# Both feed-forward openings and the second tail put under the list schedule of a decoder layer on one core

## The chip, the cores and the metric

The kernel runs on one core of one Trainium2 chip. The metric is the device time of one execution in microseconds (us). Engines are called TensorE (PE, with its weight loads PEld), VectorE (DVE), ScalarE (ACT), GpSimd (POOL) and SyncE (SP, which issues the DMAs).

## What is computed

One layer on 16 meta tokens and 1024 tokens of width 1024: a half-step SwiGLU feed-forward, a mixing stage, a second half-step feed-forward and a last norm. The core of the reference:

```python
h = h + 0.5 * swiglu(rmsnorm(h, norm_ffn1[l]), w_ffn1_gate[l], w_ffn1_up[l], w_ffn1_down[l])
u = rmsnorm(h, norm_mix[l])
qa, ka, va, qi, ki, wi, qs, ksw, vsw, ga, gb = jnp.split(u @ w_in[l], IN_SPLITS, axis=-1)
...
o_sparse = sparse_branch(qa, ka, va, qi, ki, wi, pos, kvalid, topk)
o_swa = swa_branch(qs, ksw, vsw, sinks[l], pos, kvalid)
merged = (jax.nn.sigmoid(ga) * (o_sparse @ w_branch_sparse[l])
          + jax.nn.sigmoid(gb) * (o_swa @ w_branch_swa[l]))
h = h + merged @ w_out[l]
h = h + 0.5 * swiglu(rmsnorm(h, norm_ffn2[l]), w_ffn2_gate[l], w_ffn2_up[l], w_ffn2_down[l])
return rmsnorm(h[:, BLOCK:], norm_final)

def swiglu(x, w_gate, w_up, w_down):
    return (jax.nn.silu(x @ w_gate) * (x @ w_up)) @ w_down
```

The feed-forward width is 2816, in 22 chunks of 128.

## The kernel before, in words

Activations lie transposed: eight tiles of 128 channels, the tokens in two halves x = 0 (528 columns, the 16 meta tokens among them; in the second feed-forward 512) and x = 1 (512 columns). Every float32 operand of a matmul is split into a high and a low half-precision part (`split_w` for weights, `norm_u` for the normalised rows u): ScalarE makes the high part, VectorE subtracts for the low part, and `mm3` sums three products of parts.

The function `ffn` makes one feed-forward stage. Its first pair of chunks is projected directly by `plain_pair(0)`: four weights (two gates, two ups), each by eight u tiles, for x = 0 and then x = 1; between the first halves it calls `other_half`, the norm of x = 1. From then on pairs of chunks are done with a Strassen-Winograd scheme: seven block products of half the depth (`fast`) instead of eight. Weights are combined by `wide_weights` or, for later jobs, step by step by `prepare`; the t blocks (`make_t`, `combine`) are four combinations of the normalised rows and their splits, made from rows that are computed again (`gained`) or kept (`saved`); the sixteen differences are on GpSimd. The product list `UP` is p1, p6, p7, p5, c11, p74, p53: p1 and c11 and p53 use blocks of u, the others t blocks t1 to t4. `gate_part` evicts a gate's seven products (`half_products`), `up_part` those of the up weights; `combine` on GpSimd and `split_later` make the hidden blocks for the down products. `passes` are the last projections of a stage, each followed by squares, norm and (in the second stage) the output.

In the first stage the whole of x = 0 is loaded, squared (ScalarE, added by VectorE), normalised and split; x = 1 is squared on GpSimd.

Order: the class `Plan` (a list schedule) records the operations between `start` and `run`, books each with a cost (`cost`), and issues them in planned order on the four compute engines; where it is off, operations are issued as the program says, inside a `manual_schedule` block in that order. An item's priority is its place in the program plus `shift`. Before the change only the mixing stage is planned, from `to_mix` (the last projections of the first stage included) to line 1430. `add` marks an operation as `shared` if it has two float32 inputs in SBUF; while GpSimd works such an item on VectorE is booked 0.4 us longer. Tiles in PSUM (`whole`) count as one piece for dependencies. A buffer of a ring comes free in the plan with the last use in program order.

## Time and profile before

| | us |
|---|---|
| median of 3 runs | 2007.55 (2007.2 to 2009.01) |
| the profiled execution | 2009.06 |
| its span, first to last instruction | 2007.3 |
| TensorE busy | 1922.9 (96%) |
| VectorE busy | 1630.3 (81%) |
| ScalarE busy | 898.2 (45%) |
| GpSimd busy | 385.1 (19%) |
| mean granted TensorE clock | 0.988 |

The table of stretches gives the busy time of each engine between two moments; a stretch's length minus TensorE's busy time is the time in which TensorE stood still. Groups of instructions give busy time, the mean of one and the idle time before them with what ended it. In the timeline a row is one run of like instructions: start, duration of the run, count. A duration of several matmuls holds the pipelined end of the last one, so the distance of two starts is the better price.

### The profile page before, as it was taken

The page shows a single profiled execution, that of the slowest core. Times are in us where ns is not written, and L with a number is a line of the kernel's source. Part 1 is how long each engine was busy: PE and PEld are TensorE (multiplying, and loading weights), DVE is VectorE, ACT ScalarE, POOL GpSimd, SP SyncE. Part 2 cuts the span into 40 slices and gives each one's busy share as a digit, 9 for nine tenths or more (in the row PEclk, how much of TensorE's full clock was granted, in tenths as well). Part 3 has the DMA queues.
Part 4 walks back from the last instruction along what each step waited for, and adds up shares of the span by engine and source line. Part 5 has one row for each costly group of instructions (what it writes and reads, how often), then busy time and mean ns, then how long its engine had stood idle before and what let it go on. Part 6 is the DMA issues. An engine that isn't in the chain of part 4 may idle for free.

```text
span 2007.3 us, 32840 instructions
## 1 busy us (share of the span) xinstructions
PE 1922.9 (96%) x13080; PEld 1201.4 (60%) x13080; DVE 1630.3 (81%) x2787; ACT 898.2 (45%) x1602; POOL 385.1 (19%) x313
## 2 busy tenths in 40 slices
PE   5899999999998999999999999998899999999997
PEld 4588888888887655655555656444344444444443
DVE  7988778788774899999998977566987888788767
ACT  4434233333322455669887555434333333243232
POOL 4511312221220033131000000002322213312200
PEclk9899999999999999999999999999999999999998
DMA  4011111211121554221111231341112111211213
GB/s 160 11 54 58 59 64 38 69 64 59 48 85 38 190 160 149 69 91 64 32 48 43 85 102 52 105 147 42 43 38 68 63 58 48 64 63 48 79 37 131
DMA packets 58873, 146.95 MB, mean 73 GB/s; under 512 B 7264, under 2 KB 13408, under 8 KB 58720
## 3 DMA queue, kind: packets, MB, share of 16 engines
q1 hardware_dynamic: 58720, 144.86, 22.6%
q8 instruction: 102, 1.67, 0.3%
q14 instruction: 51, 0.42, 0.1%
HBM read 130.01 MB, written 14.76 MB: 72 GB/s over the span
## 4 chain that ended last, share of the span: by engine, by line
PE 79%; DVE 12%; ACT 5%; issue 2%; DMA 1%; POOL 1%; SPq 0%; DVEq 0%; ACTq 0%; POOLq 0%
PE pc L188 15%; PE pd L188 15%; PE pa L188 15%; PE pb L188 7%; PE p_gate L326 7%; PE p_out L326 4%; PE p_br L326 3%; PE pdn L188 2%; PE ptr L326 2%; PE rp L326 2%; ACT jk L326 1%; PE pdn L326 1%; PE pv_b L326 1%; DVE wsp L326 1%; DVE sc L326 1%
## 5 line engine op out<-in xcount | busy, mean ns | idle before, releaser
L188 PEld LDWEIGHTS <-wsp 128*128 128x128 f16 x4848 | 478.0, 99 | 293.2 <-issue 30.9
L188 PEld LDWEIGHTS <-x 128*128 128x128 f16 x3132 | 307.2, 98 | 156.5 <-issue 7.0
L326 PEld LDWEIGHTS <-wsp 128*128 128x128 f16 x2448 | 235.8, 99 | 223.0 <-issue 6.9
L188 PE MATMUL pa<-u,wsp 128*128 128x264 f16 (+1 forms) x1440 | 224.7, 310 | 0.0
L326 PE MATMUL p_gate<-u,wsp 128*128 128x512 f16 x768 | 188.4, 379 | 0.0
L188 POOL TENSOR_TENSOR h<-h,base 128x512 f32<-128x512 f32 (+1 forms) x72 | 116.3, 1615 | 291.1 <-DVE base L188 229.7
L326 PE MATMUL rp<-u,wsp 128*128 128x512 f16 (+2 forms) x624 | 140.2, 366 | 4.0 <-DVE rt L326 3.7
L188 ACT ACTIVATE wsp<-wst 128x1024 f16<-128x1024 f32 (+2 forms) x88 | 80.4, 915 | 142.3 <-DMA wst<-in_wd_dram 50.4
L326 DVE SCALAR_TENSOR_TENSOR wsp<-wst,wsp 128x1024 f16<-128x1024 f32 (+2 forms) x104 | 107.5, 1036 | 27.3 <-ACT wsp L326 27.0
L188 PE MATMUL pb<-tb,wsp 128*128 128x264 f16 (+1 forms) x720 | 114.0, 312 | 8.7 <-ACT tb L188 5.9
L188 PE MATMUL pc<-tb,x 128*128 128x264 f16 (+1 forms) x720 | 114.0, 313 | 5.1 <-DVE c L188 5.0
L326 ACT ACTIVATE wsp<-wst 128x1024 f16<-128x1024 f32 (+2 forms) x104 | 91.1, 880 | 58.4 <-PE p_out L326 16.4
L188 PE MATMUL pc<-tb,wsp 128*128 128x256 f16 (+1 forms) x720 | 113.6, 313 | 0.0
L188 PE MATMUL pd<-u,x 128*128 128x256 f16 (+1 forms) x720 | 110.7, 308 | 0.0
L188 PE MATMUL pd<-tb,x 128*128 128x256 f16 (+1 forms) x720 | 110.7, 308 | 0.0
L188 POOL TENSOR_TENSOR t<-g,g 128x512 f32<-128x512 f32 x16 | 25.5, 1592 | 434.4 <-DVE g L188 434.4
L188 ACT ACTIVATE wsp<-sa 128x1024 f16<-128x1024 f32 (+1 forms) x64 | 62.3, 973 | 101.4 <-DVE sa L188 101.2
L326 ACT ACTIVATE jk<-sc,s5nb 128x784 f16<-128x784 f32 (+2 forms) x93 | 98.1, 1055 | 15.9 <-DVE s5nb L326 13.1
L188 PE MATMUL pa<-hid,wsp 128*128 128x264 f16 (+1 forms) x648 | 103.1, 310 | 0.0
L188 PE MATMUL pd<-hid,x 128*128 128x256 f16 (+1 forms) x648 | 101.6, 308 | 0.0
L188 DVE TENSOR_TENSOR c<-pc,base 128x512 f32<-128x512 f32 x80 | 55.4, 692 | 55.1 <-PE pc L188 54.8
L188 ACT ACTIVATE base<-pa 128x528 f32<-128x528 f32 (+1 forms) x64 | 38.2, 598 | 133.6 <-PE pa L188 133.6
(218 smaller groups left out, 3494.7 us busy)
## 6 DMA issues: line engine op xcount, KB each, us to landing
wst<-in_wgu_dram SPq DMA_DIRECT2D x88, 512.0 KB, 3.8
wst<-in_win_dram SPq DMA_DIRECT2D x44, 512.0 KB, 3.5
wst<-in_wd_dram SPq DMA_DIRECT2D x48, 384.0 KB, 3.5
wst<-in_wd_dram SPq DMA_DIRECT2D x32, 256.0 KB, 2.8
wst<-in_wout_dram SPq DMA_DIRECT2D x16, 512.0 KB, 3.7
qscr<-ry SPq DMA_DIRECT2D x20, 256.0 KB, 2.1
q<-qscr SPq DMA_DIRECT2D x20, 256.0 KB, 3.1
wst<-in_wbs_dram SPq DMA_DIRECT2D x16, 256.0 KB, 3.2
```

The source lines that it names most:

```text
L188: return getattr(engine.real, op)(*[give(a) for a in args], **{k: give(v) for k, v in kw.items()})
L326: getattr(engine.real, op)(*[give(a) for a in args], **{k: give(v) for k, v in kw.items()})
```

## The change

- The first stage gets a new opening, `first_pair`: three slices of tokens (272 and 256 columns of x = 0, then x = 1), each with its own squares (all on ScalarE, added on VectorE), norm and u; the four weights of the first pair take turns at every u tile; the normalised rows stay in their tiles and become the t blocks by differences on VectorE. The first slice of every h tile is loaded first, then the first weight, the second slices, the other weights (two of them into tiles of the weight sums), then x = 1.
- The first gate part of both stages is `first_gate` with the list `FIRST`: p1, p3, c11, p7, p5, p6, p74, where p3 (the product that was p53) has a bank of its own. Its evictions run with a shift of -200.
- The first stage is planned from its start to the end of that gate part; the second stage is planned from its start to the end of its first gate part, and again from its last projections to the end.
- The first two weights of the second stage are loaded and split at the end of the mixing plan (`pre`).
- The planner: `shared` counts every input that isn't a column, the surcharge is 0.5 us; matmuls into disjoint parts of one PSUM tile don't depend on each other; a buffer comes free when all its uses are done.
- A norm's Newton step is three operations instead of four.

The diff, cut:

```diff
@@ class Plan, add
-        shared = sum(v.dt == F32 and not v.base.whole for v in ins) > 1 and not any(v.base.whole for v in ins)
+        shared = sum(v.shape[1:] != (1,) for v in ins) > 1 and not any(v.base.whole for v in ins)
@@ class Plan, run
             if e == "DVE" and shared and pool_till > t:
-                busy, done = busy + 0.4, done + 0.4
+                busy, done = busy + 0.5, done + 0.5
@@ layer_kernel
     open_phase("ffn1")
     ph["S"] = 2
+    nc.start()
...
-    load_h(0)
+    CUT = 272
+    for k in range(KD):
+        nc.sync.dma_start(h[0][k][:, :CUT], xT[k][:, :CUT])
...
+    def newton(r, e, a):
+        nc.vector.scalar_tensor_tensor(e, r, -0.5, r, op0=ALU.mult, op1=ALU.mult)
+        nc.vector.tensor_mul(e, e, a)
+        nc.vector.scalar_tensor_tensor(r, e, 1.5, r, op0=ALU.add, op1=ALU.mult)
...
+        def first_products(m, blocks, first, done):
+            for what, ps in urgent(joint(blocks, FIRST)):
...
+                elif what == "p3":
+                    c12 = ftmp("c12")
+                    nc.scalar.activation(vb(c12), ps, AF.Copy)
...
+                elif what == "p5":
+                    nc.vector.tensor_add(vb(c22), ps, vb(c22))
+                    nc.vector.tensor_add(vb(c12), ps, vb(c12))
+                elif what == "p6":
+                    nc.vector.tensor_add(vb(c22), ps[:, :, :wb], vb(c22))
+                    done(3, c22, vb(c22))
+                    nc.vector.tensor_add(va(base), ps, va(base))
+                    nc.vector.tensor_add(vb(c12), va(base)[:, :, :wb], vb(c12))
...
+        def first_pair():
+            sl = ((0, 0, 272), (0, 272, 528), (1, 0, 512))
...
+            def norm_part(s, k):
...
+                nc.vector.scalar_tensor_tensor(t, hs[x][k][:, c0:c1], g_all[:, gi, k:k + 1], rb[s],
+                                               op0=ALU.mult, op1=ALU.mult)
+                nc.scalar.activation(u[x][k][:, 0, c0:c1], t, AF.Copy)
+                nc.vector.tensor_sub(u[x][k][:, 1, c0:c1], t, u[x][k][:, 0, c0:c1])
...
+            def matmuls(s, order):
...
+                for k in order:
+                    for i in range(4):
+                        mm3(ps[i // 2][:, i % 2, :width[s]], sp[i], slice(k * P, (k + 1) * P), u[x][k],
+                            slice(c0, c1), k == order[0], k == order[-1])
...
+            for i in range(4):
+                t1 = ftmp("t1")
+                a1, b1, a2, b2 = un[0][i], un[1][i], un[0][i + 4], un[1][i + 4]
+                nc.vector.tensor_sub(vb(t1), vb(b1), va(a1)[:, :, :wb])
+                nc.vector.tensor_sub(vb(b1), vb(b2), vb(b1))
+                nc.vector.tensor_sub(va(a1)[:, :, :wb], vb(b2), vb(t1))
+                nc.vector.tensor_sub(va(a2), va(a2), va(a1))
...
+        FIRST = ("p1", "p3", "c11", "p7", "p5", "p6", "p74")
+        if u is None:
+            vals, u, t_blocks = first_pair()
+            parts = [first_gate]
+        else:
+            vals = plain_pair(0)
+            parts = [first_gate]
...
-                        gates = gate_part(blocks)
+                        gates = (parts.pop() if parts else gate_part)(blocks)
+                        if nc.on:
+                            nc.run(keep=...)
...
+    raws = [load_raw(wgu1[0], 1024)]
     for k in range(KD):
+        nc.sync.dma_start(h[0][k][:, CUT:], xT[k][:, CUT:HS0[1]])
+    raws.append(load_raw(wgu1[1], 1024))
+    for i in (2, 3):
+        raws.append(new(ph["sb"], [P, 1024], F32, tag="wS", name="wst", bufs=2))
+        nc.sync.dma_start(raws[i], wgu1[i])
+    for k in range(KD):
+        nc.sync.dma_start(h[1][k], xT[k][:, HS0[1]:])
...
-    nc.run(early=6.0, keep=h2[0] + h2[1] + u3[0] + rb3 + [acc])
+    pre += [load_w(wgu2[i], 1024) for i in range(2)]
+    nc.run(early=6.0, keep=pre + h2[0] + h2[1] + u3[0] + rb3 + [acc])
     close_phase()
     open_phase("ffn2")
     ph["S"] = 1
+    nc.start()
...
-    acc = ffn(u3, rb3, h2, 2, wgu2, wd2, lambda: ffn2_norm(1, acc), passes, saved2, lambda: None)
+    acc = ffn(u3, rb3, h2, 2, wgu2, wd2, lambda: ffn2_norm(1, acc), passes, saved2, nc.start)
     x, subs, done = passes[-1]
     done(norm_stats(acc, subs))
+    nc.run(early=6.0)
```

## Rows read from the trace of the kernel before

**Rows 1.** Stretches: start:end, length, busy PE, PEld, DVE, ACT, POOL (count), clock, DMA, GB/s

```profile
0.00:114.65 114.65, 78.69 (x493) 54.98 (x494) 97.34 (x130) 52.27 (x84) 51.84 (x39) 0.94 0.24 84
...
628.00:674.00 46.00, 40.19 (x310) 30.96 (x308) 26.37 (x54) 15.20 (x27) 0.95 (x1) 0.93 0.37 117
674.00:1000.00 326.00, 309.46 (x2277) 182.35 (x2276) 315.17 (x807) 219.47 (x524) 71.64 (x77) 0.99 0.32 104
...
1359.30:1439.10 79.80, 67.77 (x292) 30.78 (x292) 65.34 (x78) 34.94 (x53) 31.62 (x20) 0.91 0.10 33
...
sum 2007.30, PE 1922.93 PEld 1201.45 DVE 1630.27 ACT 898.20 POOL 385.12; mean PE 240.37 PEld 150.18 DVE 203.78 ACT 112.28 POOL 48.14
```

**Rows 2.** Waits of PE to 115 us: in total, times, longest

```profile
PE nsum L188 <- DVE acc L188: 11.4, 1, 11.4
PE nbc L188 <- DVE n_r L188: 8.0, 2, 4.2
PE pg L188 <- DVE u L188: 6.5, 7, 2.3
```

**Rows 3.** VectorE groups by shape, to 115 us: busy us, mean ns

```profile
L188 DVE TENSOR_TENSOR u<-un,u 128x512 f16<-128x512 f32 x8 | 9.7, 1265 | 0.0
L188 DVE SCALAR_TENSOR_TENSOR wsp<-wst,wsp 128x1024 f16<-128x1024 f32 x6 | 8.9, 1484 | 0.0
L188 DVE TENSOR_TENSOR u<-un,u 128x272 f16<-128x272 f32 x8 | 8.1, 1021 | 0.1
L188 DVE TENSOR_TENSOR tb<-tu,tb 128x528 f16<-128x528 f32 x8 | 7.3, 913 | 0.5 <-ACT tb L188 0.3
L188 DVE SCALAR_TENSOR_TENSOR tu<-h,g_all,rb 128x528 f32<-128x528 f32 x8 | 5.8, 758 | 0.0
...
L188 DVE TENSOR_TENSOR acc<-acc,sq 128x528 f32<-128x528 f32 x7 | 5.0, 708 | 5.5 <-ACT sq L188 5.1
L188 DVE SCALAR_TENSOR_TENSOR tu<-h,g_all,rb 128x512 f32<-128x512 f32 x4 | 4.9, 1250 | 0.0
L188 DVE TENSOR_TENSOR tb<-t,tb 128x512 f16<-128x512 f32 x4 | 4.1, 1019 | 1.4 <-ACT tb L188 1.2
...
L188 DVE TENSOR_TENSOR u<-un,u 128x256 f16<-128x256 f32 x8 | 3.3, 419 | 0.1
...
L188 DVE SCALAR_TENSOR_TENSOR wsp<-sa,wsp 128x1024 f16<-128x1024 f32 x2 | 2.4, 1215 | 0.0
```

**Rows 4.** Timeline of VectorE: start us, us, instruction, count

```profile
72.91 0.68 DVE L188 TENSOR_TENSOR tb<-un,tb 128x512 f16<-128x512 f32 x1
```

**Rows 5.** Timeline of all engines, head of the first opening

```profile
0.74 3.93 SPq L188 DMA_DIRECT2D h<-in_xT_dram  x8
...
20.17 0.38 PE L188 MATMUL pg<-u,wsp 128*128 128x264 f16 x1 [0.20 <-ACT u L188]
```

**Rows 6.** Waits of PE in the second opening, 1359 to 1440 us

```profile
PE pb L188 <- ACT tb L188: 2.6, 1, 2.6
PE nbc L188 <- DVE n_r L188: 2.4, 1, 2.4
PE pc L188 <- DVE c L188: 2.3, 1, 2.3
```

**Rows 7.** Timeline of PE, second opening: like matmuls at two clocks

```profile
1365.24 5.34 PE L188 MATMUL pu<-u,wsp 128*128 128x512 f16 x24
...
1380.85 7.25 PE L188 MATMUL pu<-u,wsp 128*128 128x512 f16 x24
```

**Rows 8.** Table of stretches within the second opening

```profile
1359.30:1381.00 21.70, 18.51 (x89) 9.96 (x89) 9.23 (x17) 7.86 (x10) 0.00 (x0) 0.93 0.15 51
...
1400.00:1421.85 21.85, 17.70 (x79) 7.67 (x78) 21.70 (x21) 8.60 (x13) 12.98 (x8) 0.93 0.08 25
```

**Rows 9.** Timeline of PE, first opening: like matmuls at two clocks

```profile
28.11 0.86 PE L188 MATMUL pg<-u,wsp 128*128 128x264 f16 x3
...
35.71 1.96 PE L188 MATMUL pg<-u,wsp 128*128 128x264 f16 x16
```

More of the change, by code (lines that the diff above doesn't have):

```diff
@@ L112, in __init__ @@
         self.seen = []
-        self.last = self.first = None
+        self.first = None
+        self.uses, self.till = [], 0.0
     def real(self):
@@ L201, in add @@
                 for j, other, wrote in b.seen:
-                    if (write or wrote) and j != i and overlap(box, other):
+                    if (write or wrote) and j != i and (overlap(box, other) or b.whole and not (
+                            engine.name == "PE" == self.items[j][0].name)):
                         deps.add(j)
-                if write and box is None:
+                if write and (box is None or b.whole and engine.name != "PE"):
                     b.seen = []
@@ L242, in run @@
         for b in tiles.values():
-            if id(b) not in kept and b.last is not None:
-                dies[b.last].append(b)
+            if id(b) not in kept:
+                b.left = len(b.uses)
+                for i in b.uses:
+                    dies[i].append(b)
         for q in queues.values():
@@ L316, in run @@
             for b in dies[i]:
-                if b.key in free:
-                    free[b.key].append(end + 0.1)
+                b.left, b.till = b.left - 1, max(b.till, end + 0.1)
+                if b.key in free and not b.left:
+                    free[b.key].append(b.till)
                     grant(b.key)
@@ L864, in ffn @@
                     if f < NF - 2:
-                        gates = gate_part(blocks)
+                        gates = (parts.pop() if parts else gate_part)(blocks)
+                        if nc.on:
+                            nc.run(keep=hs[0] + hs[1] + u[0] + u[1][4:] + sum(t_blocks, []) + [ident, ones, g_all]
+                                   + [t for t, _ in gates] + [t for t, _ in weights[1]] + fetched[2]
+                                   + sum(down, []))
                 if not last:
```

168 lines of the change are left out of this document (133 added, 35 removed).

## The prediction

> **What bounds the kernel now.** I read the table of stretches first. TensorE works 1922.9 of the 2007.3 us (its last row), so a change of order can give back at most the 84 us in which it stands still, and the table says where these are [rows 1]: 114.65 - 78.69 = 36.0 us in the opening of the first feed-forward stage (from the start to the first product of the up part), 46.00 - 40.19 = 5.8 us where that stage passes into mixing, 326.00 - 309.46 = 16.5 us in the first half of mixing, 79.80 - 67.77 = 12.0 us in the opening of the second feed-forward stage. That is 70.3, all but some 14 us, which lie almost wholly behind the last projection. The reader is to see in the same rows that VectorE is busy 97.34 of 114.65 us in the first opening and 315.17 of 326 us in the first half of mixing: there TensorE waits because VectorE is full.
>
> Next, what TensorE waits for in the first opening [rows 2]: 11.4 us for the summed squares, 8.0 us in two waits for the inverse norm, 6.5 us for the low halves of u; all are VectorE's results. Then VectorE's work by shape [rows 3]. The point there is that one operation has two prices: the subtraction that makes the low half of u takes 419 ns at 256 columns and 1021 ns at 272, 1265 ns at 512 columns, while a subtraction of the same size elsewhere took 0.68 us [rows 4]. The dear ones lie where GpSimd works too (51.84 us in this stretch, [rows 1]): it makes the squares of the second half of the tokens and the sixteen differences for the t blocks.
>
> **First opening.** VectorE is its clock, so I keep a ledger of VectorE.
>
> Taken away. The normalised rows stay in their tiles and the t blocks are made from them, so the twelve operations that compute them again go: 5.8 + 4.9 = 10.7 us [rows 3]. GpSimd leaves this stretch but for four differences of the first hidden pair, so the surcharge goes: 8 x (1.265 - 0.68) = 4.7, 8 x (1.021 - 0.42) = 4.8, 6 x (1.484 - 1.215) = 1.6, 8 x (0.913 - 0.68) = 1.9 and 4 x (1.019 - 0.68) = 1.4, in all 14.4 us [rows 3, 4]. Together 25.1 us.
>
> Added. The sixteen differences of the t blocks move to VectorE: 16 x 0.68 = 10.9 us. All squares are now made by ScalarE and added by VectorE in three pieces: 7 x 0.42 twice and 7 x 0.68, 10.6 us, against 5.0 now, so 5.6. The first product list has seven VectorE evictions where it had five: 2 x 0.69 = 1.4. A third, small norm costs about five tiny operations, 1.0. Together 18.9 us. Net: 97.3 - 25.1 + 18.9 = 91.1 us busy.
>
> Idle time. VectorE idles 114.65 - 97.34 = 17.3 us now. The head of it shrinks: a first piece of 272 columns needs the same eight issues (3.93 us) but half the bytes [rows 5], its squares are half as long, its norm takes three blocks and not five, so the first gate matmul comes at about 13.5 us and not at 20.17 (estimate: last piece landed at 7, squares 7.8, sums 9.2, norm 10.5, broadcast 12, first u 13.5). The waits behind it are waits for a step that a list schedule can fill with weight splits. I put idle at 9. So VectorE would end at about 100 us. Of what it does, the last low halves of the next job and one hidden split (about 2.5 us) aren't needed by the gate part, since its evictions are put ahead of them. The gate part would end at 97.6 and not at 114.65: **-17 us**.
>
> Does TensorE follow? Its work at the full clock is 288 matmuls, of which 192 at 0.112 us and 96 at twice that (42 us), 168 of the gate part (18.8 us), and some 6 us for norms: 67 us from 13.5 is 80, ahead of VectorE. The new order p1, p3, c11, p7 gives it three products (8 us) that need no t block, where now the second one needs t2 (the wait of pb, 2.6 us in the second opening, [rows 6]). What is late next is thus VectorE, not TensorE. Bounds: nothing gained (half of the surcharge stays and idle stays 17.3: 91.1 + 7.2 + 17.3 = 115.6), and -24 (idle 6, three more microseconds put off).
>
> DMA queue: weights 1 to 3 are now issued behind the second pieces of h, and 2 and 3 into tiles of their own instead of waiting for a free one. Some 30 issues at 0.5 us [rows 5] are over by 16 us, and the weights are wanted from 13.5 to 21 us as VectorE splits them. I cost this at nothing; cover lost, a late weight costs its landing, some 3 us. ScalarE takes seven squares and one copy more, and is busy 52 of 115 us: nothing.
>
> **Second opening.** TensorE needs 79.8 us. Of the 12.0 us it waits, 2.6 are for t2, 2.4 for the inverse norm and 2.3 for an eviction [rows 6], the rest are shorter waits for u, t2 and the last output projection. On top, two stretches at the half clock: 24 matmuls took 7.25 us that took 5.34 before, and the clock of the whole stretch is 0.91 [rows 1, 7]; about 5 us. So 17 us could go. VectorE idles 12.5 of the first 21.7 us and is full (21.70 of 21.85) when the t blocks are due [rows 8]. The list can bring the gains of the first half (4 x 0.7 to 1.25 us) and weight sums into that early idle time, fill the norm's wait with other projections, put p3 and c11 (5.2 us) ahead of the t blocks and the evictions ahead of hidden splits. GpSimd keeps its sixteen differences here, so the surcharge stays and VectorE stays full: I take half, **-9 us**; bounds -13 and 0. The two weights split in mixing are cheap wherever they lie, under the last projections as now or in VectorE's idle 12.5 us at the head: nothing; without that cover 2 x 1.2 us [rows 3].
>
> **Mixing.** Two rules of the planner change: operations with a half-precision operand count as disturbed by GpSimd, and the surcharge booked is 0.5 and not 0.4 us; matmuls into other columns of a PSUM tile no longer order each other. The whole stage is ordered anew. The trace of before has no row for the new order. Bounds: all of the 16.5 us idle gained, or as much lost. The u row shows that such operations do pay the surcharge (1.265), so the new booking is nearer to it; I take **-1 us**.
>
> **Tail.** The newton step has three operations and not four: -0.2. The last projections run without a gap today, and their weights are split ahead of the boundary. In a region of its own they can come behind the hidden splits, as at the one boundary that is planned already, where TensorE lost 5.8 us [rows 1]. That boundary also opens new memory, this one doesn't, so I take **0**, bounds -1 and +6.
>
> **Sum.** -17 - 9 - 1 - 0.2 = -27.2 us. The profiled execution took 2009.06 us, 1.8 more than its span, and 1.5 more than the median of the runs; on the median it is 2007.55 - 27.2 = **1980.4 us**.
>
> **The rivals.**
> *TensorE at its lower clock.* Fed by VectorE in drips, TensorE may stay slow. The rows show it: three matmuls of 264 columns at 28.11 us start 0.22 us apart, the level of 1.2 GHz, sixteen at 35.71 us 0.112 apart, 2.4 GHz [rows 9]; ahead of the slow ones it had stood idle again and again. If all 192 matmuls of the first two pieces went at 0.22 it would be 13.5 + 42.2 + 20.7 + 18.8 + 6 = 101, with a wait for t about 103.5: only 11 us gained; and the second opening keeps its 5 us, 4 gained. -16.2: **1991 us**. For it: the head start is spent on exactly such drips. Against: four weights are interleaved, so each u tile brings twelve matmuls. The Trainium skill ("TensorE: Matmul & The Clock Gate", Part 1) says that the gate is at half rate unless recent activity releases it, which would speak against starting early on sparse work; by that rule the sum is this rival's. The trace agrees on the drop behind idle time.
>
> *VectorE is not relieved.* If the differences moved to it cost what it saves (the lower bound above), the first opening gains nothing; with -9 and -1 from the rest: **1997 us**. It decides if idle time stays at 17 us.
>
> *Everything fits:* -24, -13 and -4: **1966 us**.
>
> *Slower.* Mixing is the place: VectorE works 315.17 of 326 us in its first half [rows 1], so any time that a worse order costs VectorE there is paid in full. From 27 us, 8% of that stretch, it eats the gain of both openings; at 10% (33 us) the kernel takes **2013 us**. Against it: the stage's work is unchanged and the old plan's error was in the direction that is mended.
>
> **How the numbers follow.** Forecast 0.55 (its own range 1972 to 1987); lower clock 0.20; not relieved 0.07; everything fits 0.10; within 0.2% 0.03 (mixing gives back most); slower 0.05. A difference of 0.2%, 4 us, is about what a measurement here can tell from none. Faster 0.92. For eight in ten the range takes the forecast, the lower clock and part of both neighbours: 1965 to 1996, which also holds the bounds of single terms.
>
> **What would show it.** Right: first gate matmul near 13.5 us; the u subtractions at 0.69 us; first up product near 98 us, VectorE with under 10 us idle; second opening some 70 us long with VectorE still full in its middle; 674 to 1359 as long as before within 4 us; no wait over 1 us at the tail's boundary. Wrong: the low-half subtractions of u still over 1 us; TensorE at 0.22 us per matmul behind 25 us; mixing over 4 us longer.

## The result, and the profile after

The changed kernel takes 1987.33 us (median of 4 runs, 1986.49 to 1988.32), the kernel before 2007.46 us beside it (2007.2 to 2009.01): a ratio of 0.9898, 95% interval 0.9881 to 0.9915, 20.1 us less. The forecast was 1980.4 us in a range of 1965 to 1996. The profiled execution of the changed kernel took 1987.38 us, its span is 1985.3 us, 22.0 less than before.

To see where the time went, both profiled executions are cut at the same events on TensorE: the second product of the first up part ("first opening" ends; this is one product later than the end of the gate part, by which the forecast reckoned, since the first product is split by a wait after the change), the first down product, the first broadcast of the mixing stage's norm, the first gate matmul of the second stage, its second up product, the end of the last down product. All later kernels are cut in the same way.

| us | before | after | change | forecast |
|---|---|---|---|---|
| first opening | 117.35 | 94.63 | -22.7 | -17 |
| rest of the first stage | 520.72 | 520.72 | 0 | 0 |
| passage to mixing | 36.71 | 35.53 | -1.2 | 0 |
| mixing | 685.29 | 689.70 | **+4.4** | -1 |
| second opening | 81.62 | 77.47 | -4.1 | -9 |
| rest of the second stage | 549.41 | 550.68 | +1.3 | 0 |
| tail behind it | 16.20 | 16.57 | +0.4 | -0.2 |

The stretches of the profile after, which answer to [rows 1] (start:end, length, busy PE, PEld, DVE, ACT, POOL, clock, DMA, GB/s):

```profile
0.00:94.63 94.63, 74.14 (x517) 53.78 (x518) 84.10 (x158) 58.80 (x105) 6.88 (x8) 0.98 0.29 100
...
650.88:1340.58 689.70, 671.54 (x4791) 379.29 (x4792) 593.60 (x1431) 429.02 (x897) 81.54 (x117) 1.00 0.29 91
1361.00:1389.00 28.00, 26.01 (x118) 11.35 (x118) 27.12 (x30) 17.50 (x27) 18.39 (x12) 1.00 0.02 3
1389.00:1409.68 20.68, 17.63 (x74) 7.57 (x73) 20.63 (x24) 9.16 (x17) 15.33 (x9) 0.92 0.06 22
```

In the first opening GpSimd works 6.88 us where it worked 51.84, and VectorE 84.10 us where it worked 97.34 [rows 1] (99.91 up to the second up product). In the middle of the second opening VectorE has hardly any free time (27.12 of 28.00, then 20.63 of 20.68 us) and GpSimd still works beside it.

VectorE's groups by shape in the first opening after, which answer to [rows 3] (busy us, mean ns, idle before):

```profile
L334 DVE SCALAR_TENSOR_TENSOR wsp<-wst,wsp 128x1024 f16<-128x1024 f32 x5 | 6.1, 1217 | 1.8 <-ACT wsp L334 1.8
...
L334 DVE TENSOR_TENSOR tb<-tu,tb 128x528 f16<-128x528 f32 x8 | 5.3, 696 | 0.0
L334 DVE TENSOR_TENSOR u<-tu,u 128x512 f16<-128x512 f32 x8 | 5.1, 681 | 0.0
...
L334 DVE TENSOR_TENSOR tb<-t,tb 128x512 f16<-128x512 f32 x4 | 3.8, 950 | 0.0
...
L334 DVE TENSOR_TENSOR u<-tu,u 128x272 f16<-128x272 f32 x8 | 3.2, 433 | 0.0
```

Four of the five dear prices of the forecast's ledger are gone: 681 ns for 1265, 433 for 1021, 696 for 913, 1217 for 1484. The fifth stayed, 950 ns for 1019.

What TensorE waits for after, in the first opening (total, times, longest; answers to [rows 2]) and in the second (answers to [rows 6]):

```profile
PE nsb L334 <- DVE acc L334: 8.1, 1, 8.1
PE nsb L334 <- DVE n_r L334: 4.6, 1, 4.6
PE pa L189 <- DVE wsp L334: 3.8, 1, 3.8
PE pw L334 <- DVE u L334: 1.7, 2, 1.2
```

```profile
PE pa L189 <- DVE wsp L334: 4.0, 1, 4.0
PE pc L334 <- ACT tb L334: 3.0, 1, 3.0
PE pg L334 <- DVE u L334: 1.2, 2, 0.9
```

The reader is to see a wait that was not there before in either list: pa, the first up product, waits 3.8 and 4.0 us for the low half of its own weight (wsp). It stands at the end of each of the two planned openings. The wait costs more than its own length, since the granted clock falls behind it. From the first to the second up product, first the changed kernel in both stages, then the kernel before:

```profile
86.60:94.63 8.03, 4.28 (x27) 2.96 (x25) 8.03 (x12) 3.45 (x6) 0.00 (x0) 0.79 0.32 110
1409.68:1418.05 8.37, 4.36 (x14) 1.47 (x13) 8.37 (x12) 3.29 (x5) 0.00 (x0) 0.81 0.33 112
```

```profile
114.65:117.35 2.70, 2.70 (x27) 2.35 (x25) 2.56 (x5) 1.66 (x3) 0.00 (x0) 1.00 0.00 0
1439.10:1441.69 2.59, 2.59 (x13) 1.18 (x12) 2.54 (x3) 0.31 (x2) 0.00 (x0) 1.00 0.05 21
```

One product takes 8.03 us for 2.70 and 8.37 for 2.59. TensorE stood idle for 3.8 and 4.0 us, and from 90.45 and 1414.8 us on the trace has it at the level of 1.2 GHz: the granted clock is 0.79 and 0.81 there, where it was 1.00.

Gain and loss are thus in four places: the first opening, the mixing stage (which changes by the planner's rules, the Newton step and two weights at its end), the second opening, the tail. The first opening and the tail were tried by themselves and the old rules of mixing were put back; the second opening was tried by edits inside it.

### The profile page after: what moved, and what is told of

It is laid out like the page before. It is cut to its first block, busy times and chain, and to the rows that moved or that the text cites. A ratio compares the mean times of both kernels' runs of the same rounds, so it can differ in the third digit from the quotient of the medians.

```text
span 1985.3 us, 32868 instructions
## 1 busy us (share of the span) xinstructions
PE 1918.0 (97%) x13080; PEld 1196.8 (60%) x13080; DVE 1610.0 (81%) x2809; ACT 903.9 (46%) x1621; POOL 342.5 (17%) x282
## 4 chain that ended last, share of the span: by engine, by line
PE 72%; DVE 17%; ACT 6%; issue 3%; DMA 1%; SPq 0%; POOL 0%; DVEq 0%; ACTq 0%; POOLq 0%
PE pa L189 15%; PE pc L189 15%; PE pd L189 15%; PE pb L189 7%; PE p_gate L334 4%; PE p_out L334 4%; PE pdn L334 3%; DVE sc L334 3%; PE p_br L334 2%; DVE wsp L334 2%; ACT jk L334 2%; ACT psw L334 1%; DVE m L334 1%; PE rp L334 1%; DVE tb L334 1%
## 5 line engine op out<-in xcount | busy, mean ns | idle before, releaser
L189 PEld LDWEIGHTS <-wsp 128*128 128x128 f16 x4032 | 395.5, 98 | 205.7 <-DVE wsp L334 8.5
L334 PEld LDWEIGHTS <-wsp 128*128 128x128 f16 x3216 | 311.2, 99 | 295.9 <-issue 14.9
L189 PEld LDWEIGHTS <-x 128*128 128x128 f16 x3024 | 295.9, 98 | 145.1 <-issue 1.5
L189 PE MATMUL pa<-u,wsp 128*128 128x264 f16 (+1 forms) x1368 | 216.8, 313 | 7.8 <-DVE wsp L334 7.8
L334 PE MATMUL p_gate<-u,wsp 128*128 128x512 f16 x768 | 186.4, 379 | 0.0
L334 DVE SCALAR_TENSOR_TENSOR wsp<-wst,wsp 128x1024 f16<-128x1024 f32 (+2 forms) x131 | 133.1, 1019 | 38.7 <-ACT wsp L334 38.2
L334 ACT ACTIVATE wsp<-wst 128x1024 f16<-128x1024 f32 (+2 forms) x131 | 112.2, 861 | 92.3 <-PE p_out L334 28.5
L189 PE MATMUL pb<-tb,wsp 128*128 128x264 f16 (+1 forms) x684 | 106.8, 310 | 0.0
L189 PE MATMUL pc<-tb,x 128*128 128x264 f16 (+1 forms) x684 | 106.7, 310 | 0.1
L189 ACT ACTIVATE wsp<-wst 128x1024 f16<-128x1024 f32 (+1 forms) x60 | 57.9, 965 | 103.9 <-DMA wst<-in_wgu_dram 58.6
L189 PE MATMUL pc<-tb,wsp 128*128 128x256 f16 (+1 forms) x684 | 105.2, 308 | 0.0
L189 ACT ACTIVATE hid<-g 128x512 f16<-128x512 f32 (+1 forms) x54 | 33.2, 625 | 149.2 <-DVE g L189 149.2
```

The source lines that it names most:

```text
L189: return getattr(engine.real, op)(*[give(a) for a in args], **{k: give(v) for k, v in kw.items()})
L334: getattr(engine.real, op)(*[give(a) for a in args], **{k: give(v) for k, v in kw.items()})
```

## The experiments

All ratios are to the kernel before, run on the same chip; 95% intervals are about 0.0015 to each side. The kernel before took 2007.5 to 2009.7 us beside them, so that times of different kernels compare to 1 or 2 us. Stretches are cut as above. Kernels whose plan of a stretch is the same give its spread from execution to execution: 94.6 to 95.7 us for the first opening, 689.0 to 691.5 for mixing.

### The first opening alone, and mixing by the old rules

The first kernel keeps the new first opening; second opening, tail, the place of the second stage's first two weights and the planner's rules in the mixing stage are as before. The second keeps all of the change but gives the mixing stage the old rules (the surcharge and its condition, the tiles' pieces, the free rule, the old Newton step).

```diff
+        if self.mix:
+            shared = sum(v.dt == F32 and not v.base.whole for v in ins) > 1 and ...
+        else:
             shared = sum(v.shape[1:] != (1,) for v in ins) > 1 and ...
-                busy, done = busy + 0.5, done + 0.5
+                busy, done = busy + (0.4 if self.mix else 0.5), ...
+                if self.mix and b.whole:
+                    box = None
```

> Only the new opening of the first stage is kept: the mixing plan works by the old rules and with the four-operation Newton step (its order is that of the kernel before), the second stage opens and ends as before. Theory (the gain sits in the first opening, 22.7 us from the start to the second product of the up part, and some 1 us of clock at the passage to mixing): 1984 us, thus 3 us faster than the whole change; mixing from its first norm broadcast to the first projection of the second stage 685.3 us as before. Rival (the loss of 4.4 us in mixing comes from the first stage ending in another state, not from the planner's rules): 1988 us, mixing 689 to 690 us.

Measured: 1987.57 us (1987.36 to 1989.75), ratio 0.9897. First opening 94.70, mixing 686.35, second opening 82.65 us. The first opening by itself gives what the whole change gives; the other three parts together are worth nothing. Mixing went as the theory had it, the time as the rival: with its old opening the second stage gives back what mixing saves. How much of the first opening's gain is due to the slices, the order of the products, the plan or the work moved from engine to engine was not tried part by part, but for the differences below.

> The whole change, but the mixing stage planned by the old rules (surcharge 0.4 us for two float32 inputs, PSUM tiles as one piece, old release of buffers, old Newton step). Theory (the new order of mixing costs 4.4 us, the second opening gains 4.1 us): 1983 us. Rival (the two weights split ahead, or the earlier first stage, cost mixing its 4.4 us): 1987 us, mixing still near 690 us.

Measured: 1984.70 us (1984.04 to 1985.11), ratio 0.9880; mixing 686.33 us, all other stretches as in the changed kernel. So the theory held: the new rules cost the mixing stage 3.4 us, and without them the change is worth 24 us. Kernels with the old rules there have mixing at 684.9 to 687.3 us, which lies clear of the 689.0 to 691.5 with the new ones.

Where do the 3.4 us sit? Not in waits. TensorE stands still 689.70 - 671.54 = 18.2 us in mixing by the new rules and 686.33 - 667.93 = 18.4 us by the old ones; the row of the kernel with the old rules is

```profile
651.57:1337.90 686.33, 667.93 (x4790) 379.97 (x4791) 596.12 (x1433) 429.30 (x897) 81.37 (x117) 1.00 0.29 92
```

TensorE is *busy* 3.6 us longer with the same matmuls; over all traces it is busy 667.6 to 669.1 us there by the old rules and 671.4 to 673.1 by the new ones. By group, first the changed kernel, then the one with the old rules in mixing (busy us, mean ns):

```profile
L334 PE MATMUL ptr<-ident,psp 128*128 128x128 f32 x288 | 54.2, 285 | 0.9 <-DVE oT L334 0.4 <-DVE ptb L334 0.2
L334 PE MATMUL pv_b<-vt,ptb 128*128 128x64 f16 x864 | 51.1, 193 | 0.4
```

```profile
L341 PE MATMUL ptr<-ident,psp 128*128 128x128 f32 x288 | 51.7, 282 | 0.2
L341 PE MATMUL pv_b<-vt,ptb 128*128 128x64 f16 x864 | 48.2, 193 | 0.6 <-ACT ptb L341 0.3
```

The transposes and the products of 64 columns occupy the engine 2.5 and 2.9 us longer in the new order; other groups move both ways (the products p_br 96.6 us for 94.2, p_gate 186.4 for 188.4). What lies behind that is open. The ends of matmuls are modelled in the trace (the mean of 193 ns is far above the distance at which these start, 51.1 / 864 = 0.06 us), so a gap shorter than such an end counts as busy time, at every change from one kind of matmul to another: the time may be slower matmuls or small gaps between finer pieces. The number of such changes alone does not set it: it is 893 by the old rules and 946 by the new ones, but 965 in the next kernel below, where TensorE is busy 2.3 us less than in the changed one. No kernel here settles more.

### One rule at a time

The first kernel has only the surcharge and its condition as before in the mixing stage (the first two edits of the diff above), the second only this:

```diff
-        newton(r[:, :nb], e[:, :nb], a[:, :nb])
+        if nc.mix:
+            nc.vector.tensor_mul(e[:, :nb], r[:, :nb], r[:, :nb])
+            nc.vector.tensor_mul(e[:, :nb], e[:, :nb], a[:, :nb])
+            nc.vector.tensor_scalar(e[:, :nb], e[:, :nb], -0.5, 1.5, op0=ALU.mult, op1=ALU.add)
+            nc.vector.tensor_mul(r[:, :nb], r[:, :nb], e[:, :nb])
+        else:
+            newton(r[:, :nb], e[:, :nb], a[:, :nb])
```

> Only the planner's charge for a VectorE instruction beside GpSimd is put back to the old rule and to 0.4 us, and only for the mixing stage. With all four of the old rules there the mixing stage took 686.3 us, with the new ones 689.7 us. Theory: no rule is at fault by itself; a plan of some thousands of instructions comes out anew with any small difference, and its length falls anywhere within some 5 us: mixing 684 to 692 us here, and the next kernel's differs from it by more than 1 us, with neither at 686.3 by need. Rival, the dearer charge is at fault: mixing 686.3 us here, time 1984.3, and 689.7 us in the kernel with the old Newton step alone.

> Only the Newton step of the mixing stage's norms is written with its old four instructions in place of three; all planner's rules are the new ones. Theory (no rule at fault, any small difference makes a new plan): a mixing stage of another length than 689.7 us by more than 1 us, somewhere in 684 to 692 us, though the edit itself is worth 0.1 us in each of a few norms. Rival, a rule of the planner is at fault: the mixing stage stays at 689.7 us within 0.5 us and the time at 1987.3.

Measured: 1986.72 us (1986.24 to 1989.87) with mixing at 687.11, and 1986.99 us (1986.55 to 1988.38) with mixing at 687.99. The mixing stage of both:

```profile
652.82:1339.93 687.11, 669.24 (x4791) 379.40 (x4792) 593.77 (x1431) 429.75 (x897) 80.71 (x117) 1.00 0.29 92
652.03:1340.02 687.99, 668.89 (x4790) 381.02 (x4791) 594.05 (x1434) 428.18 (x897) 83.48 (x117) 1.00 0.29 92
```

Both leave the 689.0 to 691.5 of the unchanged plan, and TensorE is busy some 669 us in both; the second does so by an edit that adds an operation to each of a few norms. Either edit alone takes back most of the loss, so that a small difference is enough for another plan: the theory fits. The rival is not out, since 687.11 lies among the 684.9 to 687.3 of the old rules, so the charge alone may be the whole cause. There is one trace of each, and the medians differ from the changed kernel's by less than the runs' spread; what the other two rules do was not tried by itself.

### Sixteen differences back on GpSimd

The forecast's largest term was that GpSimd makes VectorE's instructions dear. This kernel is the changed one with the first stage's four t-block differences (times four tiles) on GpSimd again.

```diff
-                nc.vector.tensor_sub(vb(t1), vb(b1), va(a1)[:, :, :wb])
+                nc.gpsimd.tensor_sub(vb(t1), vb(b1), va(a1)[:, :, :wb])
...
```

> The sixteen differences of the first stage's t blocks go back to GpSimd, all else as changed (the mixing plan is untouched). Theory (VectorE beside GpSimd pays 0.5 to 0.6 us on each subtraction, and GpSimd needs 16 x 1.6 = 26 us for a chain that VectorE does in 10): the u and tb subtractions next to them rise from 0.68 to about 1.2 us, the first up product comes 4 to 8 us later, 1991 to 1995 us. Rival (VectorE was only loaded by moving them there): VectorE is relieved of 10 us, the up part starts 3 to 5 us earlier, 1983 us.

Measured: 1995.35 us (1990.31 to 1996.27), ratio 0.9928: the theory held, at the upper end of its range. VectorE's groups by shape in its first 96.9 us:

```profile
L334 DVE TENSOR_TENSOR u<-tu,u 128x512 f16<-128x512 f32 x8 | 11.9, 1528 | 0.0
L334 DVE TENSOR_TENSOR tb<-tu,tb 128x528 f16<-128x528 f32 x8 | 8.0, 1026 | 0.0
...
L334 DVE TENSOR_TENSOR tb<-t,tb 128x512 f16<-128x512 f32 x4 | 6.0, 1496 | 0.0
...
L334 DVE TENSOR_TENSOR acc<-acc,sq 128x512 f32<-128x512 f32 x7 | 4.8, 687 | 0.3
```

The subtraction at 512 columns costs 1528 ns, where the changed kernel has 681; the additions of the squares, which lie where GpSimd doesn't work, stay at 687. With sixteen operations taken from it VectorE is busy 85.18 us, not less than the 84.10 of the changed kernel: the surcharge, 8 x (1.528 - 0.681) + 8 x (1.026 - 0.696) + 4 x (1.496 - 0.950) + 4 x (0.946 - 0.679) = 12.7 us, is more than the 16 x 0.68 = 10.9 us that were moved. The gate part ends at 93.4 us, 6.8 later. The opening as it is cut here grew by 2.3 us only, since the next job's low halves were ready earlier in this plan (that wait is 0.6 us, and no fall of the clock follows it); the later work comes back as 1.5 us in the rest of the first stage. In this trace, the slowest of the four runs, the passage to mixing takes 3.1 us more at a lower granted clock (0.91 for 0.95), and mixing 1.8 us more, the upper end of its spread; neither is shown to come from the edit. The Trainium skill ("SBUF — State Buffer", "Who interferes with whom") says that a VectorE instruction with two inputs in SBUF contends with a GpSimd instruction that reads SBUF. The subtraction from two SBUF tiles agrees: 1528 ns in the mean beside GpSimd, 681 without.

### The same sixteen on VectorE in the second opening

```diff
-        def combine(a1, b1, a2, b2, t1):
-            nc.gpsimd.tensor_sub(vb(t1), vb(b1), va(a1)[:, :, :wb])
+        def combine(a1, b1, a2, b2, t1, eng=None):
+            eng = eng or nc.gpsimd
+            eng.tensor_sub(vb(t1), vb(b1), va(a1)[:, :, :wb])
...
-                for lst, t, n in zip(res, combine(*tiles, ftmp("t1")), WT):
+                for lst, t, n in zip(res, combine(*tiles, ftmp("t1"), nc.vector), WT):
```

> The sixteen differences of the second stage's t blocks move from GpSimd to VectorE, all else as changed. Theory (the second opening gained only 4.1 us because the surcharge stayed and the last t block comes late through GpSimd: TensorE waits 3.0 us for it): that wait goes, the u and tb subtractions fall to 0.69 us, 1983 to 1985 us. Rival (VectorE is full there anyway, so ten more microseconds on it delay the up part): 1990 to 1993 us.

Measured: 1988.63 us (1987.2 to 1989.46), ratio 0.9901; second opening 77.08 us, 0.4 less. Neither theory held. The prices fell as in the first opening (low half of u 682 ns, from 1273), and the gate part ended 3.6 us earlier (4.0 from the stage's start). But the first up product still came where it was. TensorE's timeline at the end of the region, first the changed kernel, then this one (start us, us, instruction, count, idle before):

```profile
1409.68 0.59 PE L189 MATMUL pa<-u,wsp 128*128 128x512 f16 x2
1414.29 3.96 PE L189 MATMUL pa<-u,wsp 128*128 128x512 f16 x10 [4.01 <-DVE wsp L334]
```

```profile
1406.07 0.59 PE L189 MATMUL pa<-u,wsp 128*128 128x512 f16 x2
1413.82 4.45 PE L189 MATMUL pa<-u,wsp 128*128 128x512 f16 x10 [7.16 <-DVE wsp L334]
```

The gain turned into a longer wait at the region's end, 7.2 us for 4.0. The granted clock from the first to the second up product is 0.62, where the changed kernel has 0.81. The low half of the next weight is the plan's last work for VectorE, since the gate part's evictions go ahead of it; the plan's end is what TensorE waits for.

### The next job's weights earlier

```diff
-            own = prepare(i + 1)
+            def ahead(step):
+                def run():
+                    if not nc.on:
+                        return step()
+                    was, nc.shift = nc.shift, -200
+                    step()
+                    nc.shift = was
+                return run
+            own = [(c, ahead(step)) for c, step in prepare(i + 1)]
```

> In both planned openings the steps that split the next job's weights are put ahead of their place in the plan; nothing else is changed. In the changed kernel TensorE stands 3.8 us at the end of the first opening and 4.0 us at the end of the second until VectorE has made a low half of such a weight, which the plan has as its last work. Theory: in the first opening VectorE has room (76.1 us busy of the 86.6 of the gate part), so most of the 3.8 us goes; in the second it has none (27.1 us of 28.0, then 20.6 of 20.7), so there the wait only moves into the gate part: the time comes to 1984 (1983 to 1986), the first opening to about 91.5 us, the second stays at 77 within 1 us. Rival A, the wait is the plan's order alone in both: 1979.5, second opening 73.5 us. Rival B, the weight steps delay the sums that free the PSUM tiles and the products that wait for them: 1990, first opening 97 us.

Measured: 1988.19 us (1986.73 to 1989.46), ratio 0.9894; first opening 96.58, second 74.49, rest of the second stage 552.32 us. The theory failed in both halves. In the first opening the wait for wsp is gone, but one of 3.0 us for a t block's high half stands in its place and the opening is 1 to 2 us longer, though VectorE had been idle for 10.5 us: that idle time lies at the head (9.5 of it in the first 20 us), not where the weights go. This is near the 97 us of rival B. In the second opening, where VectorE seemed too full, 3.0 us were won, and 1.6 us of them given back behind it.

### The tail

```diff
-    acc = ffn(u3, rb3, h2, 2, wgu2, wd2, lambda: ffn2_norm(1, acc), passes, saved2, nc.start)
+    acc = ffn(u3, rb3, h2, 2, wgu2, wd2, lambda: ffn2_norm(1, acc), passes, saved2, lambda: None)
     x, subs, done = passes[-1]
     done(norm_stats(acc, subs))
-    nc.run(early=6.0)
```

> The tail of the second stage is issued in the program's order, as before; both openings stay planned. From the second up product to the end of the last down product the changed kernel takes 550.7 us, a kernel with neither the second opening nor the tail planned takes 549.5 us, and the last stretch 16.6 and 15.9 us. Theory: these 1.9 us belong to the planned tail: the time comes to 1985.6, the body to 549.5 us and the last stretch to 16.0 us. Rival, they are what the second opening leaves over for the passes behind it: 1987.3, body 550.7 us.

Measured: 1986.22 us (1985.14 to 1988.78), ratio 0.9886; rest of the second stage 549.71, tail 15.92 us. The theory holds for the rest of the second stage: it takes 549.4 to 550.0 us in the kernels where the tail isn't planned and 550.6 to 551.4 where it is (early weights apart), so planning costs some 1 us. The 0.6 us of the last stretch are not shown: it takes 15.4 to 16.7 us with the plan and 15.9 to 16.2 without. More than half of the 1 us lies at the boundary, in the changed kernel (TensorE's timeline)

```profile
1924.10 1.67 PE L334 MATMUL pdn<-hid,wsp 128*128 128x512 f16 x7
1926.37 6.00 PE L334 MATMUL pdn<-hid,wsp 128*128 128x512 f16 x26 [0.60 <-DVE hid L189]
```

where the kernel without the region shows 47 such matmuls in one row, without a gap.

### The head

The first gate matmul comes at 16.92 us, not at the 13.5 of the forecast. ScalarE's timeline after shows what stands ahead of the first norm's root:

```profile
10.46 1.06 ACT L334 ACTIVATE wsp<-wst 128x1024 f16<-128x1024 f32 x1 [2.89 <-DMA wst<-in_wgu_dram]
11.53 1.28 ACT L334 ACT_TABLE_LOAD   x1
12.82 0.20 ACT L334 ACTIVATE n_r<-n_a 128x3 f32<-128x3 f32 x1
```

The root's argument is ready at 9.77 us (VectorE ends n_a there). The split of the first weight, which the list schedule put ahead, waits for its DMA until 10.46, and then the root's table is loaded.

```diff
+            first_root = small(1, "n_warm")
+            nc.scalar.activation(first_root, ones, AF.Sqrt)
             squares(0)
             norm(0)
```

> One tiny square root of the constant ones stands ahead of the first squares, so that ScalarE holds the root's table from its first load on; nothing else is changed. In the changed kernel the first norm's root waits from 9.77 us, when its argument is ready, to 12.82 us: behind the high half of the first weight (which waits for its DMA until 10.46 us and takes 1.06 us) and behind a table load of 1.28 us. Theory: the table load is on the chain that sets the first gate matmul (16.92 us), and the opening's other work hides 1.3 us nowhere, since VectorE stands idle until then: first gate matmul at 15.6 us, opening 1.3 us shorter (about 93.5 us), time 1986.0. Rival, VectorE's total sets the opening and what is won at the head is lost as idle time later: first gate matmul 15.6 us, opening 94.6 us or more, time 1987.3.

Measured: 1988.75 us (1986.06 to 1990.78), ratio 0.9894; first opening 94.81 us. This could not tell the two apart: the table load left the head, yet the first gate matmul came at 16.81 us. The root was done at 11.4, but VectorE's reciprocal stood behind the same weight's low half and began at 12.44. A sharper kernel follows below.

### Together

Three kernels add edits up. The first has the old rules in mixing, the unplanned tail and the early root, each as in the diffs above.

> The old planner's rules in the mixing stage, the tail in program order and the early root together. Each alone gave 1984.7, 1986.2 and (expected) 1986.0 against 1987.3. Theory: they lie in three stages and add up, 1984.7 - 1.1 - 1.3 = 1982.3, mixing at 686.3 us and the last two stretches at 549.7 and 15.9 us. Rival: the new order of the first opening eats the root's part, 1983.6.

Measured: 1984.43 us (1982.22 to 1985.21), ratio 0.9872. This is above the rival's time too, and no better than the old mixing rules alone (1984.70) by more than the runs' spread: neither the early root nor the unplanned tail shows in the time.

The second has besides, in the second opening, the differences on VectorE and the early weights, the latter there alone:

```diff
-                    if not nc.on:
+                    if not nc.on or ph["S"] != 1:
```

> As the kernel with the three together, and in the second opening the steps of the next job's weights early and the sixteen differences on VectorE. Early weights alone took the second opening from 77.5 to 74.5 us, and the part behind it from 550.7 to 552.3 us; the differences alone ended the gate part 3.6 us earlier, and a wait for those weights took the 3.6 us back. Theory: the two edits need each other, the second opening comes to 72 us (from 77.5) and the part behind it gives back 1.5: time 4 us below the kernel with the three. Rival, VectorE's sum of work sets the second opening whatever its order, 74.5 us, and with the 1.6 us given back the time is 1.4 us below.

Measured: **1977.27 us** (1974.78 to 1978.47), ratio 0.9837 (0.9822 to 0.9851); second opening 72.13 us, rest of the second stage 549.37. The two edits do need each other. Alone one gave 0.4 and the other 3.0 us, together 5.4 (7.0 in the third kernel, where the stretch takes 70.47 us by the same plan), and nothing is given back behind. TensorE's waits in that opening, where none is for wsp any more:

```profile
PE pc L341 <- DVE c L341: 1.7, 1, 1.7
PE pc L341 <- ACT tb L341: 1.4, 1, 1.4
PE pd L341 <- ACT tb L341: 0.7, 1, 0.7
```

The time fell by 7.2 us where theory said 4. In the profiled executions the span fell by 5.4, all of it the second opening's: mixing is 2.5 us shorter and the first opening 2.2 longer (96.10 for 93.93), both by unchanged plans. What the medians have beyond that is not explained and may be spread.

The third makes, in the plan only, the first weight's split depend on the first norm's Newton step:

```diff
             norm(0)
+            root = len(nc.items) - 1 - len(nblocks(0))
             weight(0)
+            for item in nc.items[root + 1 + len(nblocks(0)):]:
+                item[6].add(root)
```

> As the kernel with both edits of the second opening (1977.3), and in the list of the first opening the first weight's split comes behind the first norm's root on ScalarE and behind the Newton step on VectorE. In the kernel with the early root alone the table load had left the head, yet the first gate matmul came at 16.81 us and not at 16.92: the split of the first weight, whose DMA lands at 10.2 us, stands ahead of the root on ScalarE and ahead of the reciprocal on VectorE. Theory: with it behind them the inverse norm is ready at 11 us and the first gate matmul comes at 13.7 us, near the 13.5 that was forecast; VectorE's idle time in the opening falls by 2 to 3 us and the opening with it, to 93 us (from 96.1 in the kernel compared, 94 to 96 in the others); time 1974.5. Rival, what VectorE wins at the head it loses behind it (waits for the t blocks' high halves or for PSUM): first gate matmul near 13.7 us, opening 95 us or more, time 1977.

Measured: 1975.66 us (1975.38 to 1978.3), ratio 0.9835 (0.9822 to 0.9849), which can't be told from the kernel above. TensorE's timeline at the head:

```profile
11.05 1.65 PE L341 MATMUL nsb<-ident,n_r 128*128 128x16 f32 x6 [1.29 <-DVE n_r L341]
13.89 0.39 PE L341 MATMUL pw<-u,wsp 128*128 128x272 f16 x1 [1.20 <-ACT u L341]
...
17.13 7.08 PE L341 MATMUL pw<-u,wsp 128*128 128x272 f16 x40 [1.07 <-DVE wsp L341]
```

The first gate matmul comes at 13.89 us, 3 us earlier. After six matmuls TensorE waits for a weight again, VectorE is idle 10.3 us up to 91 us where it was idle 10.5 in the changed kernel, and the opening takes 93.99 us. By the plan without this edit it took 94.81, 93.93 and 96.10 us in three kernels (at granted clocks of 0.97, 0.99 and 0.95), so that a gain of 1 or 2 us can be neither shown nor shut out: 93.99 us and 1975.66 us lie between the theory and the rival. A part of what the head wins is lost a few matmuls on, since TensorE then waits for VectorE's split of the next weight (1.07 us).

Both kernels beat the changed one (ratio 0.9898) and the one before.

## Why the prediction was right, and where it was off

**The sign and the place.** VectorE set the first opening's length, and its prices fell when GpSimd left, as forecast. What is shown by experiment: the first opening alone gives the whole gain, and bringing the sixteen differences back to GpSimd costs 8 of the 20 us and raises 681 to 1528 ns. That the moved squares and the twelve operations that are no longer computed again give their part is read from the ledger, not tried.

**The sum, partly by luck.** The forecast's 1980.4 us is 6.9 below the measured median. Reckoned by its own event, the first up product, the gate part of the first stage ended at 86.60 us, 11.0 earlier than the 97.6 of the forecast (-28.0 in place of -17), and that of the second stage came 9.9 us earlier after the stage's start, near the 9 of the forecast. What the forecast had no term for is the end of each region: 5.3 and 5.8 us for the wait and the fall of the clock behind it, 11.1 us in all. That these cancel the 11.0 is luck. Mixing (5.4 us) and the end of the second stage (1.9) came out dearer, the passage 1.2 cheaper; the rest lies between the executions. Mixing over 4 us longer was one of the forecast's own signs of being wrong, and it came, with 4.4.

**First opening, -17 forecast, -22.7 measured (-28.0 to the first up product).** The ledger gave 91.1 us busy, 2.5 of them put off behind the gate part, so 88.6; the rows have 76.07 to 86.60 us, 12.5 less. Its term for the surcharge, 14.4 us, was too small. It counted five groups, of which one kept most of its price (950 ns); the trace of before has more of them, in VectorE's groups by shape to 117 us:

```profile
L188 DVE TENSOR_TENSOR sb<-wst 128x512 f32<-128x512 f32 x3 | 3.1, 1044 | 0.3 <-DMA wst<-in_wgu_dram 0.3
L188 DVE TENSOR_TENSOR sa<-sb,wst 128x512 f32<-128x512 f32 x3 | 3.0, 1016 | 0.1
...
L188 DVE TENSOR_TENSOR tb<-tu,tb 128x512 f16<-128x512 f32 x2 | 2.5, 1230 | 0.0
...
L188 DVE TENSOR_SCALAR n_e<-n_e 128x5 f32<-128x5 f32 x1 | 1.1, 1125 | 0.0
```

3 x 0.36 + 3 x 0.34 + 2 x 0.55 and the small operations of the first norm (1.13, 0.96 and 0.67 for 0.16 each, 2.3) are 5.5 us that the ledger left standing. The other mis-sized term is what the plan puts off: VectorE works without a pause for the 8.03 us behind the first up product, 5.5 more than the 2.5 of the forecast. That leaves 1.5 us open. The idle time was estimated at 9 and is 94.63 - 84.10 = 10.5 us.

**The head, 13.5 us forecast, 16.92 measured.** The step that failed is the DMA queue's, "I cost this at nothing; cover lost, a late weight costs its landing, some 3 us": the first weight lands at 10.43 us, and since its split stands ahead of the root on ScalarE and ahead of the reciprocal on VectorE, it costs the 3 us named as the bound. The head entered the sum through the idle time alone: with it mended the opening was as long, within the spread.

**TensorE at its lower clock** came, but did not last. TensorE's timeline after:

```profile
18.77 7.38 PE L334 MATMUL pw<-u,wsp 128*128 128x272 f16 x48 [1.23 <-DVE u L334]
...
26.34 5.14 PE L334 MATMUL pw<-u,wsp 128*128 128x272 f16 x43
```

From 26.34 to the next row at 31.32 us 43 matmuls start 4.98 / 43 = 0.116 us apart, the level of 2.4 GHz. Only the 15 matmuls behind 18.77 us are wide apart (0.227 us, last section), which costs 15 x 0.11 = 1.7 us in place of the rival's 21. From 22.19 us to the end of the opening the granted clock is 0.98; from 29.60 to 117.35 us it was 0.92 in the kernel before. The forecast's price of TensorE's 288 matmuls should read 43 us and not 42, without effect.

**Second opening, -9 forecast, -4.1 measured.** The forecast said itself that VectorE stays full there and took half of 17 us; the half was a choice, and to the first up product it came out at -9.9 (69.1 us for 79.0). What it did not price is the region's end, 5.8 us. The waits for the norm and for an eviction went, the one for a t block's high half stayed (3.0 us for pc, 2.6 for pb before). The stretch's clock rose from 0.91 to 0.96. Moving the differences or the weights alone left 77.1 and 74.5; both gave 72.1 and 70.5. The forecast's words that "the last low halves of the next job and one hidden split (about 2.5 us) aren't needed by the gate part" were true and misled: they are needed by the very next product, in both stages. The rival "VectorE is not relieved" has its truth in the second.

**Mixing, -1 forecast, +4.4 measured.** The bound of 16.5 us either way held; the value taken rested on no row of the new order. The argument that a truer booking gives a better order fell; with the old booking the stage takes 686.3 us. And the rival "slower" looked for the loss in VectorE's time, where it was not: VectorE is busy 593.60 us by the new rules and 596.12 by the old ones. It stands in TensorE's busy time, for a cause that is open.

**Tail, 0 forecast, some +1 measured**, inside the bounds (-1, +6). No wait above 1 us stands at the boundary, as forecast; one of 0.6 us does.

**Sum.** -22.7 - 1.2 + 4.4 - 4.1 + 1.3 + 0.4 = -21.9 us of the span. The passage's -1.2 us stands outside the change: kernels with the same code there gave 35.5 to 36.6 us, and one 38.7.

## What to carry to other kernels

When an engine's instruction shows two prices in a trace, go through all its groups and sum what the dear price costs before moving anything: here 14.4 + 5.5, some 20 us of VectorE's time by the ledger, were GpSimd's doing, and with sixteen operations moved onto it the full engine was no busier (84.10 us, 85.18 without them). A planned region has an end, and what the plan puts last is what the next instruction outside needs first; count that wait as a term of its own, with the clock behind it, and expect that relieving the region only lengthens it until the last work is moved too. A shared cost rule of a planner is a change to every stage that it plans: keep the old rule where the stage was already good, or time each stage by itself.

## What the runs showed of the hardware

Beside GpSimd's differences a VectorE instruction with two inputs in SBUF mostly pays one and the same sum, some 1.1 us, at 512 as at 1024 columns; the means of the groups mix such instructions with others. The low half of a weight (128x1024), which has a mean of 1751 ns in the second opening, took 2.29 us beside GpSimd and 1.21 with GpSimd idle; of the eight subtractions of 512 columns with the mean of 1528 ns six took 1.66 to 1.79 us, one 1.05 and one 0.68. First two rows of the changed kernel, then two of the one with the differences on GpSimd:

```profile
1387.37 2.29 DVE L334 SCALAR_TENSOR_TENSOR wsp<-sa,wsp 128x1024 f16<-128x1024 f32 x1
1415.96 1.21 DVE L334 SCALAR_TENSOR_TENSOR wsp<-sa,wsp 128x1024 f16<-128x1024 f32 x1
```

```profile
47.07 0.68 DVE L334 TENSOR_TENSOR u<-tu,u 128x512 f16<-128x512 f32 x1
62.54 1.75 DVE L334 TENSOR_TENSOR u<-tu,u 128x512 f16<-128x512 f32 x1
```

The 1265 ns of the kernel before are such a mean too: four of its eight took 1.75 to 1.78 us, one 1.03, and three 0.67 to 0.68, two of these in a pause of GpSimd. Beside GpSimd's squares the sum varies: seven subtractions of 272 columns took 0.75 to 1.52 us, where one with GpSimd idle took 0.43. Booking 0.4 or 0.5 us for every instruction is thus less than half of what most pay beside the differences, and too much for some.

Matmuls at the head start twice as far apart as later ones. In the changed kernel the 15 matmuls of 272 columns from 18.77 us on start 0.227 us apart, those behind 22.27 us 0.116; ahead of the first lay waits of 8.1, 4.6 and 1.2 us. The column of the clock shows 1.00 on both sides:

```profile
18.77:22.00 3.23, 3.23 (x15) 2.18 (x15) 3.23 (x8) 2.88 (x6) 0.00 (x0) 1.00 1.06 389
22.00:26.00 4.00, 4.00 (x36) 3.35 (x35) 4.00 (x11) 2.83 (x6) 0.00 (x0) 1.00 0.55 220
```

But the first 1.00 is no reading. The trace's records of the clock begin at 22.19 us, with the level of 2.4 GHz, and the column counts time ahead of the first record as full. In the kernel before they begin at 29.60 us, and the distance falls from 0.220 to 0.113 us between 29.46 and 29.63; in the third combined kernel they begin at 21.82, and it falls between 21.64 and 21.85. So the distance at the head is that of the level of 1.2 GHz, as the forecast read it [rows 9], and a mean clock that takes in the head is too high. DMA traffic does not set it: the column beside the clock shows 389 GB/s with the wide distance here, but in the kernel before 0 GB/s with it (25 to 30 us) and 262 GB/s with the narrow one (35.7 to 37.5). The Trainium skill ("TensorE: Matmul & The Clock Gate", Part 1) says that the clock is throttled by default and that activity releases it. The trace agrees: the level of 2.4 GHz is first on record at 22.19 us, while the matmuls run without a pause.
